# Where transfers for the sums in DRAM stand, and who issues the last features' stores and fetches

## The chip, the core and the metric

The kernel runs on one core of a Trainium2 chip. The core has TensorE (PE, matrix products into PSUM), VectorE (DVE), ScalarE (ACT), GpSimd (POOL) and SyncE (SP); 16 DMA engines move data for it. SP only issues transfers and waits for them, POOL issues transfers and does some elementwise work. Each engine works through its own instructions in order; an instruction that waits holds up all that stand behind it on its engine. The metric is the device time of one execution in microseconds, lower is better. Ahead of the change three runs gave a median of 1498.65 us (1497.84 to 1499.51).

## The reference, cut to what matters

One block on 512 tokens with 16 tokens of meta data ahead of them (528 rows, width 1024), in 32-bit floats:

```python
def swiglu(u, w_gate, w_up, w_down):            # width 1024 -> 2816 -> 1024
    return (jax.nn.silu(u @ w_gate) * (u @ w_up)) @ w_down

h = h + 0.5 * swiglu(rmsnorm(h, ffn1_norm), *ffn1)          # first feed-forward
h = h + hybrid_mixer(rmsnorm(h, mix_norm), ...)             # w_in: q, k, v, gates of both branches
h = h + 0.5 * swiglu(rmsnorm(h, ffn2_norm), *ffn2)          # second feed-forward
return rmsnorm(h, final_norm)[:, 16:]

# hybrid_mixer: retention with 4 heads (key 256, value 512, chunks of 128, decay per head),
# and attention with 8 heads of 128 over keys that an index of 8 small heads selects per query
# (top k); both pass an output matrix and a sigmoid gate, and w_mix_out joins them
```

## The kernel before, in words

**Products.** A matrix product in 32-bit precision is made of three passes: both operands are split into a high part (`whi`, made by ACT, L361) and a rest (`wlo`, made by DVE, L362), and PE sums high times high, high times rest and rest times high. A weight therefore goes the way: load by SP into `raw` (or `wq`, `w`), `whi` by ACT, `wlo` by DVE, PE. A `raw` buffer is free for the next load when DVE has made the last `wlo` from it.

**The two-by-two scheme.** The feed-forwards are computed with sums of weight quarters, so that fewer products are needed (a fast two-by-two scheme). The first feed-forward makes the sums of its weights in SBUF, with DVE (`wsum`, L528 to L534). For the second feed-forward, sums of its gate and up weights (`wsums`) and of its down weights (`dsums`) are made in DRAM by transfers alone, long before they are used. `sum_terms()` gives 48 such transfers in a fixed order: 32 for `wsums` (256x1280 floats each, 1.31 MB), then 16 for `dsums` (512x512, 1.05 MB). I number them t0 to t47. In every group of 16 there are four copies, four that add on arrival, two copies of finished sums and two additions to them, and again two and two. `next_term()` (L335 to L340) issues the next: a plain copy goes to SP's queue, one that adds goes to POOL's. An addition waits until the copy that it adds to has landed; a copy of a sum waits until the additions to that sum have landed.

**Stages.** PE's work comes in steps (a weight to load, a source, a run), and steps_through() runs them as a pipeline with the loads of later steps ahead. In the first feed-forward, steps 0 to 7 are a first downward sum; then come groups of six features each (f0 = 4, 10, 16), of 24 steps (gate and up in alternation, `psqX`, `psqY`, `psqZ` in PSUM, `g` by DVE, L582 to L596) with a downward sum of 8 steps (`psd`, `hT` by DVE, L917) behind each. The downward sum behind f0 = 4 is steps 32 to 39, that behind f0 = 10 is steps 64 to 71; from step `n_busy` = 96 the last downward sum and the projections to values follow (`psvX`, `psvZ`), up to `n_dense` = 157. Then come the retention by heads (`psrk`, `psst`, `psro`, `psrg`), the attention by heads (`psaq`, `psak`, `psao`), the output matrices, and the second feed-forward in six units with features of 14 steps each (`posts_of` puts the work beside them), its downward sums and the final norm.

**Where the terms stand before.** `with_terms(s)` puts a call of `next_term()` behind a step's run. Before, these are steps 8, 16, .. 88 (11 terms), 100, 104, .. 156 (15 terms), and every second one of the retention's steps (24 calls, of which 22 find a term left).

**What sets the order.** PE, ACT and DVE run in the order in which the code is written (BUSY engines in tc.manual_schedule). SP and POOL are ordered by the scheduler. So a moved `next_term()` moves a place in SP's and POOL's order, and PE's order stays as it was.

**Attention and features.** In the attention, the probabilities of a head are turned over by way of DRAM: POOL stores `cross` to `pd`, SP fetches `land` from it, ACT and DVE split it, and PE uses it one head later (L2049 to L2077). In the second feed-forward a unit's features go the same way: `turn()` stores to `hts`, `fetch()` gets `land`, ACT makes `hh`, DVE `hl`, and the downward sum uses them.

Of the kernel before, what the change touches and what calls it, by code (L numbers as in the profile page):

```python
# [81 lines left out]
def kernel(ctx: ExitStack, tc: tile.TileContext, x, meta, g1, wg1, wu1, wd1, gm,  # L82
                      w_in, w_ro, w_ao, w_mo, g2, wg2, wu2, wd2, gf, rope, decay, causal, out):
    nc = tc.nc
# [540 lines left out]
    if True:  # L625
# [33 lines left out]
        half = (slice(0, D // 2), slice(D // 2, D))  # L659
# [614 lines left out]
        n_dense = len(steps)  # L1274
        for i in (*range(8, n_busy, 8), *range(n_busy + 4, n_dense, 4)):
            steps[i] = with_terms(steps[i])
# [682 lines left out]
    with pool("ao") as ao:  # L1959
        vo = [ao.tile([P, AH, S], F32R, tag=f"vo{i}", name="vo") for i in range(2)]  # L1960
        ao_parts = [(vo[0][:, c, :], vo[1][:, c, :]) for c in range(AH)]
        with pool("at") as at:
# [163 lines left out]
            for h in range(AH):  # L2126
                more = h + 1 < AH
                if h == 1:
                    with tc.manual_schedule(engines=BUSY):
                        to_ones = [score(j, q, k) for j in (2, 1, 0, 3)]  # L2130
                        late_v()
                        for to_one in to_ones:
                            to_one()
                elif h:
                    scores(q, k)
# [114 lines left out]
    class Rows:  # L2250
# [67 lines left out]
        def turn(self, c, to, half):  # L2318

            src = self.room[c]  # L2320
            cross = f2["rooms"].tile([P, 1024], F32, tag=f"r{to}", name="cross")[:, : 2 * self.n].rearrange("p (b c t) -> p b c t", t=2, c=32)
            for t in range(2):
                nc.vector.transpose(cross[:, :, :, t], src[:, t].rearrange("p (b k) -> p b k", k=32))  # L2323
            d = hts[self.i % 2, half, : self.n]
            for a in range(4):
                nc.gpsimd.dma_start(d.rearrange("(b i) a e -> a i b e", i=32)[a],  # L2326
                                    cross[32 * a : 32 * a + 32].rearrange("p b c t -> p b (c t)"))

        def fetch(self, land, half):
# [6 lines left out]
            else:  # L2336
                d = d.rearrange("(k p) a e -> p k (a e)", p=P)
            tc.keep_in_program_order(nc.gpsimd.dma_start(t, d))

# [356 lines left out]
    def posts_of(u):  # L2696
# [6 lines left out]
        def put(j, *do):  # L2703
            at[j] += do

        gate_of = lambda c, half: lambda: u.silu(c, half)
        if u is u0:
# [4 lines left out]
            return at  # L2712
        a, b = (4, 6) if u.early else (3, 6)
        if u.early:
# [13 lines left out]
        put(12, lambda: u.gated("E", u.room["E"], u.room["B"], 1), lambda: u.turn("E", "D", 1), lambda: u.fetch("C", 1))  # L2728
        put(13, lambda: u.gated("A", u.d["X"], u.room["A"], 0), lambda: late.append(turn_rest))

# [48 lines left out]
    d = u4.down_steps((last_halves,))  # L2779
    woven(5, {9: d[:1], 12: d[1:2]})  # L2780
    n_units = len(steps)
# [88 lines left out]
```

## Time and profile before

| | us |
|---|---|
| median of three runs | 1498.65 |
| the profiled execution, device time | 1497.69 |
| its span, first to last instruction | 1495.9 |
| PE busy | 1473.3 (98%) |
| DVE busy | 1125.1 (75%) |
| ACT busy | 735.1 (49%) |
| POOL busy | 193.6 (13%) |
| granted TensorE clock, mean | 0.997 |

The times and rows are of one profiled execution; 1497.69 lies 0.96 below the median, inside the spread of the runs. PE is busy nearly all the time, so what counts is what makes PE wait: the waits by engine give that. A row of the timeline tells when an instruction began and how long it took, with the idle time of its engine ahead of it and what ended that in brackets. A DMA issue's last number is the time from the issue to the landing, which includes what is queued ahead of it. In windows, "PEclk" is the granted clock as a share of 2.4 GHz.

### The profile page before, as it was taken

The page shows a single profiled execution, that of the slowest core. Times are in us where ns is not written, and L with a number is a line of the kernel's source. Part 1 is how long each engine was busy: PE and PEld are TensorE (multiplying, and loading weights), DVE is VectorE, ACT ScalarE, POOL GpSimd, SP SyncE. Part 2 cuts the span into 40 slices and gives each one's busy share as a digit, 9 for nine tenths or more (in the row PEclk, how much of TensorE's full clock was granted, in tenths as well). Part 3 has the DMA queues.
Part 4 walks back from the last instruction along what each step waited for, and adds up shares of the span by engine and source line. Part 5 has one row for each costly group of instructions (what it writes and reads, how often), then busy time and mean ns, then how long its engine had stood idle before and what let it go on. Part 6 is the DMA issues. An engine that isn't in the chain of part 4 may idle for free.

```text
span 1495.9 us, 22481 instructions
## 1 busy us (share of the span) xinstructions
PE 1473.3 (98%) x8800; PEld 1306.3 (87%) x8800; DVE 1125.1 (75%) x1736; ACT 735.1 (49%) x1048; POOL 193.6 (13%) x272
## 2 busy tenths in 40 slices
PE   9999999999999999999999999999999999999997
PEld 8999999999887888989898888898888878888885
DVE  4987586686785876777979788778456768897886
ACT  5655254364353444453333437767534645555453
POOL 1000000002210212101101032233001300101110
PEclk9999999999999999999999999999999999999999
DMA  5177533536959879585837644656744656866852
GB/s 171 59 217 204 169 105 103 177 115 166 359 130 357 252 209 269 184 239 165 218 116 211 165 121 119 179 168 178 255 157 141 222 174 217 272 199 222 266 172 99
DMA packets 185594, 281.29 MB, mean 188 GB/s; under 512 B 15120, under 2 KB 113576, under 8 KB 184848
## 3 DMA queue, kind: packets, MB, share of 16 engines
q1 hardware_dynamic: 161856, 209.20, 42.5%
q0 software_dynamic: 20096, 64.35, 18.0%
q10 hardware_dynamic: 3536, 6.31, 1.2%
q8 instruction: 69, 1.13, 0.3%
q14 instruction: 37, 0.30, 0.1%
HBM read 249.66 MB, written 88.88 MB: 226 GB/s over the span
## 4 chain that ended last, share of the span: by engine, by line
PE 81%; DVE 8%; DMA 7%; ACT 2%; issue 2%; SPq 0%; POOLq 0%; POOL 0%; ACTq 0%; DVEq 0%
PE psqX L2368 7%; PE psro L157 6%; PE psqX L157 5%; PE psrg L157 5%; PE psd L157 5%; PE psga L157 3%; PE psat L157 3%; PE psvX L1219 3%; PE psqY L2368 3%; PE psmo L157 3%; PE psak L157 3%; PE psqY L157 3%; PE psaq L157 3%; PE psdX L2430 3%; PE psrk L157 3%; DVE wlo L362 2%
## 5 line engine op out<-in xcount | busy, mean ns | idle before, releaser
L361 ACT ACTIVATE whi<-raw 128x1024 fp32r<-128x1024 f32 (+2 forms) x143 | 134.0, 940 | 117.3 <-PE psd L157 37.2
L362 DVE TENSOR_TENSOR wlo<-raw,whi 128x1024 fp32r<-128x1024 f32 (+2 forms) x143 | 157.8, 1107 | 31.3 <-ACT whi L361 31.2
L362 DVE TENSOR_TENSOR wlo<-wq,whi 128x1024 fp32r<-128x1024 f32 x76 | 92.1, 1216 | 39.6 <-ACT whi L361 39.5
L361 ACT ACTIVATE whi<-wq 128x1024 fp32r<-128x1024 f32 x76 | 80.0, 1060 | 58.3 <-PE psdX L2430 12.7
L157 PE MATMUL psro<-vo,whi 128*128 128x512 f32 x256 | 78.9, 389 | 0.0
L157 PE MATMUL psd<-hl,whi 128*128 128x264 f32 x352 | 71.2, 284 | 0.0
L157 PE MATMUL psd<-hh,wlo 128*128 128x264 f32 x352 | 70.9, 283 | 0.0
L157 PE MATMUL psd<-hh,whi 128*128 128x264 f32 x352 | 70.6, 282 | 0.0
L117 ACT ACTIVATE whi<-raw 128x1024 fp32r<-128x1024 f32 (+1 forms) x44 | 45.4, 1037 | 49.5 <-PE psat L157 17.3
L118 DVE TENSOR_TENSOR wlo<-raw,whi 128x1024 fp32r<-128x1024 f32 (+1 forms) x44 | 53.8, 1222 | 20.6 <-ACT whi L117 20.5
L157 PE MATMUL psqX<-th,whi 128*128 128x264 f32 x216 | 61.3, 284 | 3.8 <-DVE g L596 3.8
L157 PE MATMUL psqX<-tl,whi 128*128 128x264 f32 x216 | 61.1, 283 | 0.0
L157 PE MATMUL psqX<-th,wlo 128*128 128x264 f32 x216 | 61.1, 283 | 0.0
L157 PEld LDWEIGHTS psro<-vo,whi 128*128 128x128 f32 x256 | 48.0, 188 | 10.2
L157 PEld LDWEIGHTS psd<-hh,wlo 128*128 128x128 f32 x352 | 54.4, 188 | 0.0
L157 PEld LDWEIGHTS psd<-hh,whi 128*128 128x128 f32 x352 | 54.3, 188 | 0.0
L157 PEld LDWEIGHTS psd<-hl,whi 128*128 128x128 f32 x352 | 53.9, 188 | 0.0
L2326 POOL DMA_DIRECT2D hts<-cross x40 | 26.5, 693 | 199.5 <-DVE cross L2323 199.4
L361 ACT ACTIVATE whi<-wsum 128x1024 fp32r<-128x1024 f32 x36 | 38.1, 1059 | 28.4 <-PE psd L157 15.0
L157 PE MATMUL psrg<-xh,whi 128*128 128x512 f32 x128 | 50.5, 394 | 0.0
L157 PE MATMUL psrg<-xl,whi 128*128 128x512 f32 x128 | 49.9, 390 | 0.0
L157 PE MATMUL psrg<-xh,wlo 128*128 128x512 f32 x128 | 49.9, 389 | 0.0
(610 smaller groups left out, 4760.4 us busy)
## 6 DMA issues: line engine op xcount, KB each, us to landing
wq<-wsums SPq DMA_DIRECT2D x40, 512.0 KB, 4.5
raw<-in_w_in_dram SPq DMA_DIRECT2D x18, 1024.0 KB, 5.9
raw<-in_w_in_dram SPq DMA_DIRECT2D x33, 512.0 KB, 4.1
w<-in_w_in_dram SPq DMA_DIRECT2D x24, 512.0 KB, 9.0
raw<-in_ffn_w_up_dram SPq DMA_DIRECT2D x11, 1024.0 KB, 5.0
raw<-in_ffn_w_gate_dram SPq DMA_DIRECT2D x10, 1024.0 KB, 5.9
wsums<-in_ffn_w_up_dram POOLq DMA_DIRECT2D x8, 1280.0 KB, 11.1
wsums<-wsums SPq DMA_DIRECT2D x8, 1280.0 KB, 10.8
```

The costliest lines, as they stand in the source:

```text
L117: nc.scalar.activation(hi, src, AF.Copy)
L118: eng.tensor_tensor(lo, src, hi.bitcast(F32), ALU.subtract)
L157: nc.tensor.matmul(o, a[:, k, :], b[:, sl], start=first and k == 0 and i == 0, stop=last and k == nk - 1 and i == 2, skip_group_check=onto)
L361: nc.scalar.activation(hi, src, AF.Copy)
L362: return lambda: nc.vector.tensor_tensor(lo, src, hi.bitcast(F32), ALU.subtract)
L1219: nc.tensor.matmul(d[bank_][t], a, b[:, k, :], start=not onto and j + k + m == 0, stop=j + k == 3 and m == 2, skip_group_check=onto)
L2326: nc.gpsimd.dma_start(d.rearrange("(b i) a e -> a i b e", i=32)[a], cross[32 * a : 32 * a + 32].rearrange("p b c t -> p b (c t)"))
L2368: nc.tensor.matmul(ps[:, t], a, b[:, k, :], start=not onto and j + k + m == 0, stop=j + k == 3 and m == 2, skip_group_check=onto)
L2430: nc.tensor.matmul(ps[:, t], a, b[:, k, :], start=not onto and k + m == 0, stop=k == 1 and m == 2, skip_group_check=onto)
```

## The change

1. In the first feed-forward and the values' stage the terms stand elsewhere: behind steps 32, 34, 36, 38 and 64, 66, 68, 70 (two downward sums, 8 terms) and behind steps 106, 112, .. 154 (9 terms). The retention's 24 calls stay, and issue t17 to t40. A new `next_term()` at the head of each attention head issues t41 to t47.
2. In the second feed-forward's last unit (`i == 5`) the stores of half 0 and both fetches go to SP's queue in place of POOL's, and `turn_rest` runs in step 13 and not behind the next step.
3. In its unit 1 the tiles for the hidden features and half 1 of them come at step 5 in place of 4, and half 0 at step 7 in place of 6.
4. The first downward step that is woven into the last unit stands behind step 10 in place of 9.

```diff
@@ -1272,7 +1272,7 @@
         steps += units[1].steps(units[2], rope_beside(ret_k, slice(0, T))) + [gate_step(OFF_GR + P, 1)]
         steps += units[2].steps(None, rope_beside(ret_q, REAL))
         n_dense = len(steps)
-        for i in (*range(8, n_busy, 8), *range(n_busy + 4, n_dense, 4)):
+        for i in (*range(32, 40, 2), *range(64, 72, 2), *range(n_busy + 10, n_dense, 6)):
             steps[i] = with_terms(steps[i])
         pipe = steps_through(steps)
         with tc.manual_schedule(engines=BUSY):
@@ -2125,6 +2125,7 @@
             pend = None
             for h in range(AH):
                 more = h + 1 < AH
+                next_term()
                 if h == 1:
                     with tc.manual_schedule(engines=BUSY):
                         to_ones = [score(j, q, k) for j in (2, 1, 0, 3)]
@@ -2322,9 +2323,10 @@
             for t in range(2):
                 nc.vector.transpose(cross[:, :, :, t], src[:, t].rearrange("p (b k) -> p b k", k=32))
             d = hts[self.i % 2, half, : self.n]
+            queue = nc.sync if self.i == 5 and half == 0 else nc.gpsimd
             for a in range(4):
-                nc.gpsimd.dma_start(d.rearrange("(b i) a e -> a i b e", i=32)[a],
-                                    cross[32 * a : 32 * a + 32].rearrange("p b c t -> p b (c t)"))
+                queue.dma_start(d.rearrange("(b i) a e -> a i b e", i=32)[a],
+                                cross[32 * a : 32 * a + 32].rearrange("p b c t -> p b (c t)"))
 
         def fetch(self, land, half):
             d = hts[self.i % 2, half, : self.n]
@@ -2335,7 +2337,7 @@
                 t = t.rearrange("p (h k) e -> p h k e", h=2)
             else:
                 d = d.rearrange("(k p) a e -> p k (a e)", p=P)
-            tc.keep_in_program_order(nc.gpsimd.dma_start(t, d))
+            tc.keep_in_program_order((nc.sync if self.i == 5 else nc.gpsimd).dma_start(t, d))
 
         def new_hidden(self, make):
             self.hid = [make(c) for c in "hl"]
@@ -2710,7 +2712,7 @@
             put(2, lambda: split_t(3), lambda: new_t(4), lambda: squares(1), lambda: squares(2), lambda: squares(3), token_norm)
             put(3, load_gf, lambda: split_t(4), u.gates, lambda: late.append(u.turned))
             return at
-        a, b = (4, 6) if u.early else (3, 6)
+        a, b = (5, 7) if u.early else (3, 6)
         if u.early:
             put(a, lambda: prev.new_hidden(plain_tile), lambda: late.append(prev.hidden(1)))
         else:
@@ -2726,7 +2728,7 @@
         put(9, lambda: u.add("E", "X"))
         put(11, lambda: u.add("B", "Y"), lambda: late.append(gate_of("B", 1)))
         put(12, lambda: u.gated("E", u.room["E"], u.room["B"], 1), lambda: u.turn("E", "D", 1), lambda: u.fetch("C", 1))
-        put(13, lambda: u.gated("A", u.d["X"], u.room["A"], 0), lambda: late.append(turn_rest))
+        put(13, lambda: u.gated("A", u.d["X"], u.room["A"], 0), (lambda: turn_rest()) if u.i == 5 else lambda: late.append(turn_rest))
 
         def turn_rest():
             u.turn("A", "B", 0)
@@ -2777,7 +2779,7 @@
         tail_w.extend(split_w(raw[:, i : i + 2, :]) for i in (0, 2))
 
     d = u4.down_steps((last_halves,))
-    woven(5, {9: d[:1], 12: d[1:2]})
+    woven(5, {10: d[:1], 12: d[1:2]})
     n_units = len(steps)
     c0, c1 = [], []
     add_steps(d[2:])
```

The three places that follow are of SP and POOL. An `x3` stands for three equal rows.

SP, first feed-forward, from the last gate and up loads of f0 = 4 over its downward sum into f0 = 10. Before:

```order
L133 DMA raw<-in_ffn_w_gate_dram 128x8x256
L133 DMA raw<-in_ffn_w_up_dram 128x8x256
L339 DMA wsums<-in_ffn_w_gate_dram 256x1280
L133 DMA raw<-in_ffn_w_down_dram 128x6x256 x3
L339 DMA wsums<-in_ffn_w_gate_dram 256x1280
L133 DMA raw<-in_ffn_w_down_dram 128x6x256
L133 DMA raw<-in_ffn_w_gate_dram 128x8x256
L133 DMA raw<-in_ffn_w_up_dram 128x8x256
```

And now:

```order
L133 DMA raw<-in_ffn_w_gate_dram 128x8x256
L133 DMA raw<-in_ffn_w_up_dram 128x8x256
L133 DMA raw<-in_ffn_w_down_dram 128x6x256 x3
L339 DMA wsums<-in_ffn_w_up_dram 256x1280
L133 DMA raw<-in_ffn_w_down_dram 128x6x256
L339 DMA wsums<-in_ffn_w_up_dram 256x1280
L133 DMA raw<-in_ffn_w_gate_dram 128x8x256
L339 DMA wsums<-in_ffn_w_gate_dram 256x1280 x2
L133 DMA raw<-in_ffn_w_up_dram 128x8x256
```

The copies t0 to t2 are gone from among the gate and up loads of f0 = 4 (the last of them is the third row before); all four first copies stand at the downward sum, one more of them ahead of the next gate load and two ahead of the next up load.

SP, end of the retention, with the semaphores that a row waits for (DMAHW: a transfer of SP's, DMASW: one of POOL's). `raw` loads are of the output matrix of the retention and of w_in. Before, around the loads `raw_8365` and `raw_8413`:

```order
L133 DMA raw_8070<-in_w_in_dram 128x8x128 [waits DMAHW1_49,DVE_49]
L133 DMA raw_8163<-in_w_ret_out_dram 128x4x512 [waits DMAHW2_49,DVE_49]
L339 DMA dsums_91<-dsums_91 512x512 [waits DMASW1_49]
L133 DMA raw_8278<-in_w_ret_out_dram 128x4x512 [waits DMAHW6_49,DVE_49]
L133 DMA raw_8365<-in_w_in_dram 128x8x128 [waits DMAHW7_49,DVE_49,Activation_49]
L133 DMA raw_8413<-in_w_in_dram 128x8x256 [waits DMAHW3_49,DMAHW1_49,DVE_49]
L339 DMA dsums_91<-dsums_91 512x512 [waits DMAHW4_49,DMASW6_49]
L133 DMA raw_8491<-in_w_in_dram 128x8x128 [waits DMAHW5_49,DMAHW2_49,DVE_49]
L1441 DMA vraw_8923<-vst_82 128x2048 [waits DVE_49]
```

And now:

```order
L339 DMA dsums_91<-in_ffn2_w_down_dram 512x512 [waits DMAHW1_49]
L133 DMA raw_8061<-in_w_in_dram 128x8x128 [waits DMAHW5_49,DVE_49]
L133 DMA raw_8154<-in_w_ret_out_dram 128x4x512 [waits DMAHW6_49,DMAHW3_49,DVE_49]
L339 DMA dsums_91<-in_ffn2_w_down_dram 512x512
L133 DMA raw_8269<-in_w_ret_out_dram 128x4x512 [waits DMAHW2_49,DVE_49]
L339 DMA dsums_91<-in_ffn2_w_down_dram 512x512
L339 DMA dsums_91<-dsums_91 512x512 [waits DMAHW7_49,DMASW3_49]
L133 DMA raw_8356<-in_w_in_dram 128x8x128 [waits DMAHW0_49,DMAHW3_49,DVE_49,Activation_49]
L133 DMA raw_8404<-in_w_in_dram 128x8x256 [waits DMAHW5_49,DMAHW1_49,DVE_49]
L339 DMA dsums_91<-in_ffn2_w_down_dram 512x512
```

Three copies from the down weights and a copy of a sum (t41, which waits with DMASW3 for an addition on POOL's queue) now stand ahead of the two loads `raw_8356` and `raw_8404`, which were `raw_8365` and `raw_8413`; before, one copy of a sum stood there, whose addition had been issued earlier.

POOL, attention, between the stores of two heads, as a difference:

```order
 L2049 DMA pd<-cross 32x16x128 x2
-L2051 DMA land_9134<-crosst 16x16
+L2051 DMA land_9127<-crosst 16x16
 L1411 DMA vtail<-vd 16x4x128 x3
+L339 DMA dsums<-in_ffn_w_down_dram 512x512
 L2049 DMA pd<-cross 32x16x128
 L1335 TENSOR_TENSOR tmp<-tmp,sin 128x512
```

An addition stands ahead of the next head's stores and of the product with the sine; three more stand at other heads, where before the attention had none, and on SP two copies of sums stand behind the fetches of two heads.

## Rows read from the trace of the kernel before

**Rows 1.** The page's section 1: busy time by engine, share of the span, instructions.
```profile
PE 1473.3 (98%) x8800; PEld 1306.3 (87%) x8800; DVE 1125.1 (75%) x1736; ACT 735.1 (49%) x1048; POOL 193.6 (13%) x272
```

**Rows 2.** Waits of PE: who waited for whom, total us, times, longest us.
```profile
PE psqX L157 <- DVE g L596: 3.8, 2, 2.0
PE psvZ L1219 <- DVE wlo L362: 2.9, 1, 2.9
PE psd L2613 <- DVE hl L362: 2.1, 1, 2.1
PE psqX L2368 <- ACT u L2304: 1.4, 1, 1.4
```

**Rows 3.** Windows of the values' stage: length, busy by engine, PEclk, DMA share, GB/s.
```profile
474.00:478.00 4.00, 1.14 (x6) 0.60 (x4) 3.68 (x4) 2.08 (x2) 0.00 (x0) 1.00 1.03 402
478.00:480.00 2.00, 2.00 (x7) 1.58 (x8) 1.97 (x2) 0.00 (x0) 0.00 (x0) 0.71 1.00 359
480.00:482.00 2.00, 2.00 (x9) 1.15 (x11) 2.00 (x3) 0.00 (x0) 0.00 (x0) 0.50 1.05 366
```

**Rows 4.** SP's timeline, first feed-forward: start, length, what.
```profile
154.04 0.54 SPq L339 DMA_DIRECT2D wsums<-in_ffn_w_gate_dram  x1
164.05 0.37 SPq L133 DMA_DIRECT2D raw<-in_ffn_w_gate_dram  x1
176.51 0.37 SPq L133 DMA_DIRECT2D raw<-in_ffn_w_up_dram  x1
```

**Rows 5.** DMA issues at 80.8, 80.4, 88.7, 91.9 us: KB, us to landing.
```profile
wsums<-in_ffn_w_up_dram SPq DMA_DIRECT2D x1, 1280.0 KB, 7.6
raw<-in_ffn_w_up_dram SPq DMA_DIRECT2D x1, 1024.0 KB, 4.9
wsums<-in_ffn_w_up_dram POOLq DMA_DIRECT2D x1, 1280.0 KB, 11.0
raw<-in_ffn_w_gate_dram SPq DMA_DIRECT2D x1, 1024.0 KB, 10.3
```

**Rows 6.** DVE's timeline (three rows), then ACT's (one), where these loads are used.
```profile
174.20 0.69 DVE L528 TENSOR_TENSOR wsum<-raw 128x512 f32<-128x512 f32 x1 [2.48 <-DMA raw<-in_ffn_w_gate_dram]
179.58 0.77 DVE L917 SCALAR_TENSOR_TENSOR hT<-psd,hT 128x264 f32<-128x264 f32 x2 [0.68 <-PE psd L157]
183.90 0.77 DVE L917 SCALAR_TENSOR_TENSOR hT<-psd,hT 128x264 f32<-128x264 f32 x2 [1.81 <-PE psd L157]
186.84 0.64 ACT L361 ACTIVATE whi<-raw 128x512 fp32r<-128x512 f32 x1 [0.99 <-PE psqZ L157]
```

**Rows 7.** DMA issues in the values' stage at 465.45, 510.88, 512.83 us.
```profile
raw<-in_w_in_dram SPq DMA_DIRECT2D x1, 1024.0 KB, 20.4
wsums<-wsums SPq DMA_DIRECT2D x1, 1280.0 KB, 12.0
raw<-in_w_in_dram SPq DMA_DIRECT2D x1, 1024.0 KB, 27.0
```

**Rows 8.** Retention's end: SP's row, two landings, then ACT, DVE, PE's psst.
```profile
794.80 0.37 SPq L133 DMA_DIRECT2D raw<-in_w_ret_out_dram  x1
raw<-in_w_ret_out_dram SPq DMA_DIRECT2D x1, 1024.0 KB, 8.7
dsums<-in_ffn_w_down_dram POOLq DMA_DIRECT2D x1, 1024.0 KB, 10.2
818.53 1.04 ACT L361 ACTIVATE whi<-raw 128x1024 fp32r<-128x1024 f32 x1
820.75 0.70 DVE L362 TENSOR_TENSOR rqk<-tmp,rqk 128x528 fp32r<-128x528 f32 x1
L1565 PE MATMUL psst<-rqk x30: 170/286/389, 827.1 to 831.1; 128*128 128x512 f32 x6, 128*128 128x400 f32 x6, 128*128 128x272 f32 x6, 128*128 128x256 f32 x6
```

**Rows 9.** The page's section 6: the 512 KB loads of w_in.
```profile
raw<-in_w_in_dram SPq DMA_DIRECT2D x33, 512.0 KB, 4.1
```

**Rows 10.** ACT's timeline in the second feed-forward's unit 1.
```profile
1202.64 0.66 ACT L361 ACTIVATE hh<-land 128x512 fp32r<-128x512 f32 x1 [5.56 <-DMA land<-hts]
```

## The prediction

> **What bounds the kernel now.** First the busy times: PE is busy 98% of the span [rows 1], no other engine comes near, and the clock is full. So the change can only take away time in which PE waits, or add to it. Second, the waits of PE [rows 2]: in the first feed-forward two of about 2 us for `g`, in the values' stage one of 2.9 for a `wlo`, in the second feed-forward one of 1.4 for `u` and, near the end, one of 2.1 for `hl`. These are all that the moved work can win by name. Third, the windows behind the wait in the values' stage [rows 3]: PE works only 1.14 of the 4 us from 474, and then the granted clock falls to 0.71 and 0.50, the lower level of 1.2 GHz, for 4 us. At 2.00 x 0.29 and 2.00 x 0.50 that is 1.6 us more. I put 1.6 behind every new wait that is longer than 2.9 us too.
>
> PE's order is the same but for one pair of steps, so the whole question is when weights land. The timeline of SP and the landings tell that [rows 4, 5]: a 1 MB load alone lands in 4.9 us, a copy of 1.31 MB alone in 7.6, an addition in 11.0, and a load issued beside an addition in 10.3.
>
> **First feed-forward.** Removed: t0 to t2 from among the gate and up loads of f0 = 4. With them go the two waits of [rows 2], if they come from late loads (10.3 in place of 4.9, and DVE in order behind them): 3.8 us, taken in full.
>
> Added: in its downward sum and behind it four copies rather than one, and POOL issues the addition to each as soon as its copy has landed. A last term in this place was t3, issued at 154.04; the next gate load was issued at 164.05 and the next up load at 176.51 [rows 4]. DVE already waits 2.48 us for the gate load, at 174.20 [rows 6], and what it does next is in a fixed order: the `hT` sums that free PE's banks are behind it. Between there and 184 it has only 0.68 + 1.81 = 2.5 us idle.
> - Gate: one more copy (t1) is queued ahead of it on SP. That costs between 0 (it fits in before 164.05) and 12.0, a copy beside an addition [rows 7]. I take 6, nearer to the 7.6 of a copy alone since part of t1 runs ahead of the gate's issue: the gate lands at about 180, and PE is 6 - 2.5 = 3.5 late.
> - Up: behind the gate come t2, t3 and then the load, with the additions to t1 and t2 beside them. A load behind two copies took 20.4 us, a load behind one copy and beside two additions 27.0 [rows 7]. Counted from the gate's landing at 180 the first gives 200, the second with another copy of 7.6 gives 215; a start at 176.51 with 20.4 gives 197. I take 203, nearer to two copies, as the additions start only one by one. ACT wants these weights at 186.84 [rows 6], by now 3.5 later, 190.3; some 2 us lie between ACT and PE (its idle 0.99 and DVE's like). PE waits 203 - 190.3 - 2 = 10.7; ends 5 and 23.
> - With the clock's 1.6: 3.5 + 10.7 + 1.6 - 3.8 = +12.0, ends +1 and +29.
>
> The second four (steps 64 to 70) are additions only; POOL has nothing ahead of them, so they don't run in the second downward sum but at about 162 to 215, as above. The later downward sums get nothing.
>
> A rule stands against that price: the Trainium skill, "DMA: Bandwidth & Descriptors", section "Queues, rings and completion order", says that every DMA engine takes turns packet by packet between the queue rows that have work. By even turns a load beside an addition would take at most twice 4.9, that is 9.8; the trace has 10.3 although the addition ended 7.8 us after the load's issue, so the load got rather less than half. By even turns the up load would be some 5 us earlier, and the whole sum 5 us lower.
>
> **Values' stage.** With 9 terms in place of 15 fewer copies stand ahead of its loads. The wait of 2.9 and its 1.6 of clock [rows 2, 3] should go: -4.5, ends -4.5 and 0 (another transfer lands late there).
>
> **Start of the retention.** t17 stands ahead of a few small loads. I take +0.5, ends 0 and +2, from one 7.6 us copy of which the stage's other work covers most.
>
> **End of the retention.** The third copy is issued right behind the load of 794.80, which landed after 8.7 [rows 8], at 803.5; the copy lands with 7.6 at 811. Its addition on POOL takes 10.2, so 821.3. Only then SP passes t41 and issues `raw_8356`, behind t41's copy: 7.6 and some 1 for the load, 830. ACT split that load at 818.53, DVE ended `rqk` behind it at 821.4 and PE began `psst` with it at 827.1 [rows 8]: 5.7 us of cover. PE is late by 830 - 818.5 - 5.7 = 5.8. The two additions ahead of that one in POOL's queue can add up to 10.2; I take 2. With the clock's 1.6: +9.4; ends 0 (POOL's additions come earlier) and +17. What is queued behind SP's wait is just this: the load of the gate's weights and the next, and behind them the split on ACT and DVE, which hold `psst` and `psro`'s sums.
>
> **Attention.** It gains two copies on SP ahead of 512 KB loads, which land in 4.1 otherwise [rows 9], and four additions beside the stores and fetches of the turned heads. Loads are used as soon as they are there. From below the cost is 0 (PE uses a head's probabilities a head later), from above twice a copy's 7.6 less some 2 of cover each, 11. I take +4: a load behind a copy some 4 late, half of it covered, and as much for an addition beside a fetch.
>
> **Second feed-forward, unit 1.** ACT sat idle for 5.56 until a fetch landed at 1202.64 and only then made what `u` waits for [rows 10]. Now a split stands ahead of that, which gains its 1.04 (a pass of the kind in [rows 8]); but the second fetch stands behind one more weight load on SP, which waits for a buffer. That is one split by ACT and one by DVE, 2.3 together. +1.5; ends -1.4 (the wait of [rows 2] goes) and +2.5.
>
> **Tail.** The stores and fetches of half 0 go to SP, in step 13 itself; the fetch now stands behind the tail's weights. DVE makes `hl` of half 1 behind its work on `hTok` as before, so the 2.1 stays. +0.5; ends -2.1 and +1.5. The Trainium skill, same page, section "Issuing engines are not separate DMA queues", holds that the choice of the issuing engine saves issue time alone; no row here shows more.
>
> **Sum.** 12.0 - 4.5 + 0.5 + 9.4 + 4 + 1.5 + 0.5 = +23.4. On the profiled 1497.69 that is 1521.1; the median stands 0.96 above it. I predict 1521.
>
> **The rivals.**
> - *The loads still come in time* (faster). The downward sums load little (768 KB a step), and if the copies run in that gap, the price at both places is gone. Then -3.8 - 4.5 - 1.4 and at best -2.1 remain: 1487 to 1490. It decides at a gate landing before 177 and an up landing before 190. For it: the first downward sum had one term without a wait of PE. Against it: DVE's 2.48 [rows 6]. 0.12.
> - *Only the first feed-forward pays*: t41's addition is done in time. 12.0 - 4.5 + 0.5 + 4 + 2 = +14, 1512. 0.16.
> - *Only the later stages pay*: the first four copies are absorbed. -3.8 - 4.5 + 0.5 + 9.4 + 4 + 2 = +7.6, 1506. 0.10.
> - *Nothing to be measured*: gains of 8.3 against as much loss. 1498. 0.07.
> - *The terms aren't where the code says*: if POOL held the additions until steps 64 to 70, the up load would lie beside none, land at 197, and 6 us less be lost: 1515, inside my case's range.
>
> **How the numbers follow.** My case, 1513 to 1537, has 0.55. The range 1499 to 1537 takes in it and the two partial cases, and leaves out faster, most of the case at 1498, and some 0.05 above. Faster by over 0.2% (3 us, about what a measurement of this kernel can tell from no change): 0.12; within: 0.07; slower: 0.81.
>
> **What would show it.** In the changed kernel's waits of PE: `g` gone from f0 = 4; a wait of about 3 near 180 and one of about 11 near 192 to 203, with PEclk below 1 behind it; none at 474; one of 6 to 10 at the last head's `psst`, with SP's issue of t41 near the landing of an addition; small ones in the attention. If the landing of the gate and up loads is as before (174 and 181), the largest term is wrong; if SP passes t41 before 812, the second.

## The result, and the profile after

The changed kernel takes 1518.84 us (median of 4 runs, 1517.3 to 1520.39), the kernel before beside it 1498.36 (4 runs, 1497.84 to 1499.51). The ratio is 1.0136 with a 95% interval of 1.0118 to 1.0153: slower by 1.4%. A second measurement, beside three of the later experiments, gave 1.0130 (1.0111 to 1.0148). The prediction was 1521, with 1513 to 1537 for its likeliest case.

The profiled execution of the changed kernel takes 1517.43 with a span of 1515.6, against 1497.69 and 1495.9. The page's busy times, to be held against [rows 1]:

```profile
PE 1480.4 (98%) x8800; PEld 1307.9 (86%) x8800; DVE 1126.7 (74%) x1736; ACT 735.0 (48%) x1048; POOL 188.1 (12%) x266
```

PE's busy time grew by 7.1 us although it does the same work. The lower clock behind its waits, which the windows below show, accounts for about half of that: the mean granted clock is 0.994 in place of 0.997, some 4 us on 1473 (an estimate); the rest of the 7.1 is not traced. The other 12.6 of the 19.7 are waits of PE. The longest of them, to be held against [rows 2] (who waited for whom, total us, times, longest us):

```profile
PE psd L157 <- DVE wlo L362: 6.9, 1, 6.9
PE psqX L2370 <- ACT u L2305: 3.2, 1, 3.2
PE psd L2615 <- DVE hl L362: 2.6, 2, 2.1
PE psst L1565 <- DVE accr L1844: 2.4, 2, 1.7
PE psqX L157 <- DVE g L582: 2.1, 1, 2.1
PE psao L2077 <- DVE ptl L118: 1.8, 4, 0.8
```

The two waits for `g` of [rows 2] and the one of `psvZ` are gone, and so is a shorter one of 1.3 for `psn` ahead of the latter. In their place stand one of 6.9 for a `wlo` in the first feed-forward, one of 2.1 for `g` (now L582), 3.2 in place of 1.4 for `u`, and a row of small ones in the retention (`psst`) and the attention (`psao`, `psS`).

PE's order is the same in both kernels but for one pair of steps in the tail, so the start of the same instruction in both traces tells how late PE is at each place. The stages come out like this:

| from | start before | start after | PE late by | change in the stage | predicted |
|---|---|---|---|---|---|
| first feed-forward, from 6 us (0.8 late there) | 127.48 | 124.39 | -3.1 | -3.9 | -3.8 |
| its downward sum, gate load | 181.54 | 186.82 | 5.3 | +8.4 | +3.5 |
| its next up load | 194.78 | 204.04 | 9.3 | +4.0 | +10.7, and 1.6 of clock |
| values' stage: `psn` | 384.08 | 392.04 | 8.0 | -1.3 | 0 |
| values' stage: `psvZ` | 482.01 | 485.29 | 3.3 | -4.7 | -4.5 |
| start of the retention | 577.94 | 582.63 | 4.7 | +1.4 | +0.5 |
| end of the retention | 829.51 | 837.58 | 8.1 | +3.4 | +9.4 |
| attention | 1061.87 | 1078.80 | 16.9 | +8.9 | +4 |
| second feed-forward, unit 1 | 1207.85 | 1228.19 | 20.3 | +3.4 | +1.5 |
| tail | 1487.32 | 1506.88 | 19.6 | -0.7 | +0.5 |

The largest term first. SP's issues at the first feed-forward's downward sum (start, length, what), in place of [rows 4]:

```profile
153.24 0.57 SPq L339 DMA_DIRECT2D wsums<-in_ffn_w_up_dram  x1
160.85 0.37 SPq L133 DMA_DIRECT2D raw<-in_ffn_w_gate_dram  x1
161.27 8.10 SPq L339 DMA_DIRECT2D wsums<-in_ffn_w_gate_dram  x2
183.77 0.37 SPq L133 DMA_DIRECT2D raw<-in_ffn_w_up_dram  x1
```

POOL's in the same stretch, with what ended the idle time before them:

```profile
158.96 1.01 POOL L339 DMA_DIRECT2D wsums<-in_ffn_w_up_dram  x1 [117.20 <-DMA wsums<-in_ffn_w_up_dram]
166.71 0.90 POOL L339 DMA_DIRECT2D wsums<-in_ffn_w_up_dram  x1 [6.74 <-DMA wsums<-in_ffn_w_up_dram]
185.20 0.87 POOL L339 DMA_DIRECT2D wsums<-in_ffn_w_up_dram  x1 [17.59 <-DMA wsums<-in_ffn_w_gate_dram]
188.14 0.88 POOL L339 DMA_DIRECT2D wsums<-in_ffn_w_up_dram  x1 [2.07 <-DMA wsums<-in_ffn_w_gate_dram]
```

The gate load was issued at 160.85. The addition to t0 had started at 158.96 and the one to t1 followed at 166.71. DVE's rows say when the load was there, and when DVE came to the `wlo` that the longest wait of PE is for:

```profile
181.46 0.69 DVE L528 TENSOR_TENSOR wsum<-raw 128x512 f32<-128x512 f32 x1 [12.95 <-DMA raw<-in_ffn_w_gate_dram]
182.79 0.95 DVE L362 TENSOR_TENSOR wlo<-raw,whi 128x768 fp32r<-128x768 f32 x1
```

That is 12.95 us of waiting where [rows 6] has 2.48. The load took 20.6, by far longer than the 10.3 of [rows 5]; the `wlo` of a down weight for which PE waits, and the `hT` sums, which free PE's banks, stand behind it in DVE's order. The next up load, which waits for the same `wlo` to free a buffer, could then only be issued at 183.77 and landed after 13.4:

```profile
raw<-in_ffn_w_up_dram SPq DMA_DIRECT2D x1, 1024.0 KB, 13.4
```

Windows of the changed kernel (window, length, busy time of PE, PEld, DVE, ACT, POOL, then PEclk, DMA share, GB/s):

```profile
176.00:184.00 8.00, 1.14 (x9) 0.93 (x9) 2.50 (x4) 2.06 (x2) 0.00 (x0) 0.77 1.03 349
184.00:186.00 2.00, 2.00 (x10) 2.00 (x11) 2.00 (x4) 0.05 (x1) 0.80 (x1) 0.50 0.91 356
198.00:201.00 3.00, 0.92 (x7) 0.81 (x7) 3.00 (x5) 1.13 (x3) 0.00 (x0) 0.97 1.03 208
201.00:203.00 2.00, 2.00 (x11) 2.00 (x11) 2.00 (x4) 0.97 (x2) 0.00 (x0) 0.50 0.95 250
831.00:835.00 4.00, 2.35 (x11) 1.64 (x10) 3.97 (x8) 1.06 (x1) 0.00 (x0) 1.00 1.05 381
1226.00:1228.00 2.00, 2.00 (x6) 1.56 (x5) 1.90 (x3) 2.00 (x3) 0.00 (x0) 0.50 0.30 37
```

In the first, PE works 1.14 us of 8 while the DMA engines are full (1.03). Behind it the clock is 0.50, the lower level of 1.2 GHz, as in [rows 3]; behind the second wait (198 to 201) again. At 831, in the retention, waits that are shorter leave it at 1.00. The last is of the second feed-forward, behind 3.2 us of waiting: 0.50.

### The profile page after: what moved, and what is told of

It is laid out like the page before. It is cut to its first block, busy times and chain, and to the rows that moved or that the text cites. A ratio compares the mean times of both kernels' runs of the same rounds, so it can differ in the third digit from the quotient of the medians.

```text
span 1515.6 us, 22484 instructions
## 1 busy us (share of the span) xinstructions
PE 1480.4 (98%) x8800; PEld 1307.9 (86%) x8800; DVE 1126.7 (74%) x1736; ACT 735.0 (48%) x1048; POOL 188.1 (12%) x266
## 4 chain that ended last, share of the span: by engine, by line
PE 79%; DMA 8%; DVE 7%; issue 2%; ACT 2%; SPq 1%; POOL 0%; POOLq 0%; ACTq 0%; DVEq 0%
PE psd L157 7%; PE psqX L2370 7%; PE psqX L157 7%; PE psvX L1219 4%; PE psro L157 4%; PE psqY L157 3%; PE psrq L157 3%; PE psat L157 3%; PE psqY L2370 3%; PE psmo L157 3%; PE psrg L157 3%; PE psrk L157 2%; PE psga L157 2%; PE psvY L1219 2%; PE psdX L2432 2%
## 5 line engine op out<-in xcount | busy, mean ns | idle before, releaser
L361 ACT ACTIVATE whi<-raw 128x1024 fp32r<-128x1024 f32 (+2 forms) x143 | 134.2, 941 | 125.3 <-PE psd L157 34.1
L157 PE MATMUL psro<-vo,wlo 128*128 128x512 f32 x128 | 49.8, 389 | 0.0
## 6 DMA issues: line engine op xcount, KB each, us to landing
wsums<-in_ffn_w_up_dram POOLq DMA_DIRECT2D x8, 1280.0 KB, 13.4
```

The costliest lines, as they stand in the source:

```text
L157: nc.tensor.matmul(o, a[:, k, :], b[:, sl], start=first and k == 0 and i == 0, stop=last and k == nk - 1 and i == 2, skip_group_check=onto)
L361: nc.scalar.activation(hi, src, AF.Copy)
```

## The experiments

All times are medians, each with its ratio to the kernel before in the same call. The kernel before took 1498.18 beside the first eight terms alone, the additions left out, the terms later and unit 1 as before; 1497.34 beside the attention's additions left out, the two kernels with 9 terms and the changed kernel again; 1495.55 beside the last four. In the last all its runs but one lie between 1492.4 and 1499.7, so that differences of a tenth of a per cent stay open. Against the changed kernel, which ran in the second of these calls alone, the others are compared by their ratios.

**One part alone: the first eight terms.** The kernel before, with

```diff
-        for i in (*range(8, n_busy, 8), *range(n_busy + 4, n_dense, 4)):
+        for i in (*range(32, 40, 2), *range(64, 72, 2), *range(72, n_busy, 8), *range(n_busy + 4, n_dense, 4)):
```

> The kernel before with one edit: t0 to t7 stand behind steps 32, 34, 36, 38 and 64, 66, 68, 70 of the first feed-forward (as in the changed kernel) and t8 to t10 stay at steps 72, 80, 88; nothing else of the program is touched. Theory (the four copies and their additions at the downward sum hold up the next gate and up loads; that is a loss by itself): PE's start after that place was 9.3 - 0.7 = 8.5 us later in the changed kernel, so about 1498.5 + 8.5 = 1507, with a wait of PE psd for wlo near 180 of about 7 us and none for g at 103 and 126. Rival (the loss is given back later, since PE's delay gives the loads of the values' stage and the retention more time): the wait at 475 shrinks or goes and the time is 1500 to 1503.

Measured: 1503.87, ratio 1.0046 (1.0022 to 1.0069), 5.7 us (3.3 to 10.3 by the interval). Its waits of PE:

```profile
PE psd L157 <- DVE wlo L362: 5.7, 1, 5.7
...
PE psvZ L1219 <- DVE wlo L362: 1.6, 1, 1.6
```

The wait near 180 is there by itself, with one of 1.3 for `g` near 209. From 6 us to 216 us PE loses 5.9 us, in the changed kernel's first trace 8.6, in its second 5.9; behind 475 the wait was 1.6 in place of 2.9, and 1.1 us is given back there. The time lies between the two theories' ranges, nearer to the rival's (up to 1503) than to 1507, and its interval takes in both. The trace shows the loss by itself, and little of it given back.

**The additions left out.** The changed kernel, with t4 to t7 not issued:

```diff
+    left_out = [terms[i] for i in range(4, 8)]
...
-            dst, src, add = terms.pop(0)
+            term = terms.pop(0)
+            if any(term is t for t in left_out):
+                return
+            dst, src, add = term
```

> The changed kernel with the additions t4 to t7 left out (the first four terms that add on arrival are not issued, so the sums lack a part); the copies t0 to t3 stand where they stood. Theory (the additions on POOL's queue, which start as each copy lands, take the DMA engines from the gate load behind them: it was issued at 160.9 and landed 181.4, 1.5 after the second addition landed at 179.9): without them the gate load lands by 172, PE's waits near 180 and 198 (6.9 and 2.1 us) and the low clock behind them go, and 8.4 + 4.0 = about 12 us are gone, 1506 to 1508. Rival (the copies on SP's own queue ahead of and behind the load are enough): the gate load still lands after 178 and the time is 1516 to 1519.

Measured: 1504.54, ratio 1.0048 (1.0031 to 1.0066), against 1.0130 with them: 12.3 us (13.2 by the first measurement's 1.0136). The same two copies t2 and t3 land like this (KB, median us), first in the changed kernel, then without the additions:

```profile
wsums<-in_ffn_w_gate_dram SPq DMA_DIRECT2D x2, 1280.0 KB, 24.8
```

```profile
wsums<-in_ffn_w_gate_dram SPq DMA_DIRECT2D x2, 1280.0 KB, 11.8
```

And DVE took up the gate load without waiting for it, 7.6 after its issue at 160.09, so that it landed within 7.6 at most:

```profile
167.67 0.68 DVE L532 TENSOR_TENSOR wsum<-raw 128x512 f32<-128x512 f32 x1
```

The instruction of PE that starts at 204.04 in the changed kernel, and at 194.78 before, starts at 190.82 here. So the copies on SP's queue alone cost nothing here, four of them with two loads among them and one behind: what costs is the additions, which start of themselves as each copy lands. The theory holds.

Why an addition holds up a load so much, the DMA queues show. While the gate load of the changed kernel lay beside additions (166.8 to 179.8), then in this kernel (160.1 to 167.6); q0 is POOL's queue, q1 SP's (packets, MB, share of the 16 engines' time):

```profile
q0 software_dynamic: 425, 2.01, 77.5%
q1 hardware_dynamic: 931, 1.07, 25.7%
```

```profile
q1 hardware_dynamic: 1419, 2.86, 100.4%
```

SP's queue moved 1.07 MB in 13 us beside the additions and 2.86 MB in 7.5 us without them. Beside them it still moved more than twice as many packets as POOL's, but had a quarter of the time: a packet of an addition kept an engine busy for about 0.38 us, one of SP's for 0.06 (estimates from these rows: the share of the time, times the window, times 16 engines, divided by the packets).

**The attention's additions left out.** The same edit with `(42, 43, 46, 47)`:

> The changed kernel with the four additions of the attention left out (t42, t43, t46 and t47 are not issued, so the second and fourth sums of the down weights lack a part); the three copies stand where they stood. Theory (the additions, 10 to 12 us each on the DMA engines, hold up the fetches of the turned heads, which took 7 to 9 us beside them in place of 3 to 4, and PE's start was 7 us later between 1015 and 1065, where the last two lie): 1518.8 - 7 = about 1512, and no wait of psao for ptl over 0.5. Rival (the two copies on SP, which stand behind the fetches and ahead of the weight loads, are the cause): no more than 2 us are gone, 1517.

Measured: 1509.59, ratio 1.0086 (1.0069 to 1.0103), 7.4 less than with them. The fetches of a turned head in the changed kernel, beside the last addition; then before; then here, beside none (KB, median us to landing):

```profile
dsums<-in_ffn_w_down_dram POOLq DMA_DIRECT2D x1, 1024.0 KB, 11.9
land<-pd SPq DMA_DIRECT2D x2, 256.0 KB, 8.8
```

```profile
land<-pd SPq DMA_DIRECT2D x2, 256.0 KB, 2.7
```

```profile
land<-pd SPq DMA_DIRECT2D x2, 256.0 KB, 2.7
```

8.8 in place of 2.7. Against the changed kernel's run in the same call, PE's start was 0.0 apart at 837 and 7.8 earlier at 1064. The additions are the cause. Against the kernel before, PE is 8.0 late here at 831 and 7.2 at 1062, so that the two copies on SP, which I had weighed equally, cost nothing that this trace shows.

**The same terms later.** `next_term()` taken out of the heads' loop and put into the loop over the column blocks of the attention's output matrix:

> The changed kernel with t41 to t47 issued behind the attention, one at each column block of the attention's output matrix, in place of one at each attention head. That takes t41's copy, which waits for an addition, from ahead of two weight loads at the end of the retention, and two copies and four additions out of the attention. Theory (they cost about 3 us at the retention's end and 8.9 us in the attention, where PE got later by so much): 1518.8 - 12 = about 1507, with at most 3 more if the output matrix stage pays for them. Rival (the attention's delay comes from elsewhere, or the copies cost as much behind the attention, where the second feed-forward's first weights are loaded): 1514 to 1519.

Measured: 1513.44, ratio 1.0116 (1.0091 to 1.0141). In the trace 2.9 us go at the retention's end (SP no longer waits with t41 there) and 8.0 in the attention, as expected, but 9 of these 11 come back within 70 us, most of it at one place:

```profile
PE psao L2077 <- ACT pth L117: 5.2, 1, 5.2
```

A copy, issued at 1044.20, now stands ahead of the last head's fetches, and an addition, issued at 1046.73, lies beside them; which of the two makes them late was not tried. The theory held for what was taken out, the rival for where it was put.

**Unit 1 as before.** The changed kernel with

```diff
-        a, b = (5, 7) if u.early else (3, 6)
+        a, b = (4, 6) if u.early else (3, 6)
```

> The changed kernel with the posts of the second feed-forward's unit 1 as before (hidden tiles and half 1 at step 4, half 0 at step 6). Theory (the later steps let one more weight load go ahead of the second fetch, so that u, which ACT makes behind hh, comes late: PE waits 3.2 in place of 1.4, and the clock falls to 0.50 behind it): the PE wait for u is back at 1.4 and 3.4 us are gone, 1515.4. Rival (the longer wait comes from the whole stage lying 17 us later against its transfers, not from the posts): 1518 to 1519 with a wait of 3 for u.

Measured: 1513.59, ratio 1.0112 (1.0081 to 1.0143), 2.7 us less than the changed kernel's 1.0130 by the ratios, whose intervals overlap. The trace is plainer; its wait for `u`:

```profile
PE psqX L2370 <- ACT u L2305: 0.9, 1, 0.9
```

0.9 in place of 3.2, and PE's lead over the changed kernel grows by 3.9 us at just this place. In the changed kernel ACT's row, to be held against [rows 10], is

```profile
1222.39 0.66 ACT L361 ACTIVATE hh<-land 128x512 fp32r<-128x512 f32 x1 [6.50 <-DMA land<-hts]
```

This speaks for the posts, but doesn't show that they are the whole. With the posts as changed the wait for `u` was 3.4 in the second trace of the changed kernel, 2.4 and 2.0 in the two kernels without additions and 1.7 with the attention's terms later; with the posts as before it runs from 0.9 here to 2.2 in the kernels below. What else sets it was not tried.

**A version that beats both, first try.** The one gain of the change lies in the values' stage. The kernel before, with 9 terms there and the last four at the mix output product:

```diff
-        for i in (*range(8, n_busy, 8), *range(n_busy + 4, n_dense, 4)):
+        for i in (*range(8, n_busy, 8), *range(n_busy + 10, n_dense, 6)):
...
-        steps += [(*mo_raw(c), lambda w, lower, c=c: mo_run[0](c, w, lower)) for c in range(KD)]
+        steps += [(*mo_raw(c), lambda w, lower, c=c: (mo_run[0](c, w, lower), next_term())) for c in range(KD)]
```

> The kernel before with three of its places changed: the values' stage has 9 terms as in the changed kernel (steps n_busy + 10, + 16, ..) in place of 15, the first feed-forward keeps its 11, the retention's 24 calls all find a term (before: 22), and the last four terms (two copies, two additions) are issued by the steps of the mix output product. Theory (the one gain that the changed kernel showed is the values' stage: the waits at 382 and 475 and the low clock behind the latter, 1.3 + 4.7 = 6 us; a few terms more are free where no load is needed at once): 1492 to 1495 where the kernel before has 1498. Rival (every moved term costs elsewhere about what it gained): 1497 to 1501.

Measured: 1512.54, ratio 1.0099 (1.0084 to 1.0114). PE was 7.6 us early at 482, so the gain is there (some of it is a wait for `g` that is missing from this trace, though the first feed-forward's terms stand as before); but then come these waits of PE:

```profile
PE pspv L1586 <- ACT wt L1343: 12.4, 1, 12.4
PE psro L157 <- ACT vo L361: 3.7, 1, 3.7
```

With fewer terms ahead the retention begins with four additions, all issued within 3 us, where the kernel before has two. What lay beside them (KB, us to landing):

```profile
wsums<-in_ffn_w_up_dram POOLq DMA_DIRECT2D x4, 1280.0 KB, 23.0
raw<-in_w_in_dram SPq DMA_DIRECT2D x1, 1024.0 KB, 34.1
```

A load of 1 MB takes 34.1. The terms at the mix output product cost nothing. My theory missed that the later terms change their kind at every place when their count ahead changes.

**The same, by the gate loads.** `range(12, n_busy, 8)` in place of `range(8, n_busy, 8)`:

> As values_9_terms, and the 11 terms of the first feed-forward four steps later (steps 12, 20, .. 92 in place of 8, 16, .. 88), so that a copy follows a gate load and its addition lies beside the next up load. Theory (an addition beside any gate or up load makes that land in 10 in place of 5, and DVE and PE wait for it in either case): the two waits for g of 2 us stay in another place, time as values_9_terms within 2. Rival (up loads have cover that gate loads lack): those waits go and it is 4 lower.

Measured: 1515.27, ratio 1.0115 (1.009 to 1.0141). Both theories fail in part:

```profile
PE psqX L157 <- DVE g L582: 3.3, 2, 2.2
```

The waits at 103 and 126 went, and others came near 137 and 310. Nor did it save the 4 us: 1.0115 against 1.0099. What makes the difference is seen in the next kernel, which shares this place.

**The smallest moves.** From that, three kernels with the first two terms at steps 12 and 20, all else as before; then with t17 two steps later too (`124` to `126`); then, in place of that, two terms fewer in the values' stage.

> The kernel before with two terms moved: t0 and t1 stand behind steps 12 and 20 in place of 8 and 16, so that each copy follows a gate load and its addition lies beside the up load behind; t2 to t47 stay. Theory (an up load has cover that a gate load lacks, and the third addition was free where it lay, in the downward sum): the two waits for g near 103 and 126 (3.8 us) go and nothing takes their place, 1494.5 where the kernel before has 1498.2. Rival (what the waits hide comes up elsewhere, as in values_9_terms_by_gate, where a wait came near 139): 1497 to 1499.

Measured: 1495.7, ratio 1.0002 (0.9989 to 1.0016). No change, by the rival: a wait for `g` of 2.5 stands near 136 in place of the two, and the one in the values' stage stays:

```profile
PE psqX L157 <- DVE g L582: 2.5, 1, 2.5
...
PE psvZ L1219 <- DVE wlo L362: 2.0, 1, 2.0
```

SP's and POOL's issues there, and DVE's row behind the second addition:

```profile
100.17 0.38 SPq L133 DMA_DIRECT2D raw<-in_ffn_w_up_dram  x1
110.37 0.37 SPq L133 DMA_DIRECT2D raw<-in_ffn_w_gate_dram  x1
...
121.57 0.37 SPq L133 DMA_DIRECT2D raw<-in_ffn_w_up_dram  x1
```

```profile
101.78 1.02 POOL L339 DMA_DIRECT2D wsums<-in_ffn_w_up_dram  x1 [61.12 <-DMA wsums<-in_ffn_w_up_dram]
120.54 0.89 POOL L339 DMA_DIRECT2D wsums<-in_ffn_w_up_dram  x1 [17.74 <-DMA wsums<-in_ffn_w_up_dram]
```

```profile
133.25 0.69 DVE L528 TENSOR_TENSOR wsum<-raw 128x512 f32<-128x512 f32 x1 [4.60 <-DMA raw<-in_ffn_w_up_dram]
```

The first addition (101.78) began when the up load of 100.17 was on its way and was all but over when the gate load was issued at 110.37: nothing waited. The second (120.54) began 1.0 us ahead of an up load, DVE waited 4.60 for it, and PE with it. So here it is no matter of gate or up: an addition of 10 to 11 us nearly fills the time from one load to the next; the one that began behind a load's issue was free, the one that began ahead of it was not.

> As two_terms_by_gate, and t17 behind step 126 in place of 124 (two steps after n_busy + 28), so that its copy stands behind a pair of weight loads of the values' stage and no longer ahead of them. Theory (the wait of 2.9 near 475 and the low clock behind it, 4.6 us in all, come from this one copy queued ahead of the late load): 3.8 + 4.6 = 8.4 less than the kernel before, 1490. Rival (it takes fewer terms, as with 9 of them, since the additions beside do it too): the wait stays above 1.5 and the time is 1493 to 1495.

Measured: 1494.43, ratio 0.9986 (0.9973 to 1.0). The wait of `psvZ` is gone, with one copy moved by two steps; PE gains 2.3 us there on the kernel above. The one for `g` is as in that kernel, 2.6. The two differ in nothing else, so in these traces it was that one copy. The kernel has the lowest median of all here, 1.1 us below the kernel before, at the edge of what can be told.

> As two_terms_by_gate, and the values' stage has 13 terms (none behind steps 124 and 128), all later terms two calls later, so that the retention begins with the copies t24 and t25 and every one of its 24 calls finds a term. Theory (the order of the terms at the retention's edges decides: with copies at its start and four additions not at once, the waits of 12.4 and 3.7 us of values_9_terms don't come): 1491 to 1495. Rival (any shift of the retention's terms makes one of its loads late): over 1498 with a wait of pspv, psst or psro above 2.

Measured: 1504.64, ratio 1.0064 (1.0043 to 1.0084), by the rival. A copy now stands ahead of `u`, the retention's decay, beside two additions; PE's wait and DVE's row:

```profile
PE psst L1565 <- DVE tmp L1569: 11.5, 1, 11.5
```

```profile
581.58 1.17 DVE L1569 TENSOR_TENSOR tmp<-psst,u 128x512 f32<-128x512 f32 x2 [17.24 <-DMA u<-in_decay_dram]
```

**The tail's edits on top.** The kernel with three terms moved, with half 0's stores and both fetches by SP, `turn_rest` at once and the weave at step 10:

> As three_terms_moved, and the changed kernel's edits of the second feed-forward's last unit (half 0's stores and both fetches by SP, turn_rest in its own step, the first woven downward step behind step 10), without those of unit 1. Theory (in the changed kernel PE's start fell back by 0.7 us in the tail, so they are worth that or nothing): as three_terms_moved within 1. Rival (the fetches queue behind the tail's weights and cost 1.5): 1 to 2 slower.

Measured: 1495.07, ratio 0.9994 (0.998 to 1.0009): within 1 of the kernel without them, as expected; they are worth nothing that can be told, either way.

**The changed kernel again**, beside the kernels of the second call:

> The changed kernel again, on the same chip and beside the same runs of the kernel before as the three that follow. Every theory: 1517 to 1520, ratio about 1.0136; the length of the wait near 180 may differ by 2 us from run to run, since it hangs on how the transfers share the DMA engines.

Measured: 1517.02, ratio 1.0130. The wait near 180 was 5.7 in place of 6.9. At the end of the retention PE waited 3.4 at once, and there the clock fell too:

```profile
833.00:836.00 3.00, 2.70 (x6) 2.15 (x7) 2.96 (x6) 0.54 (x1) 0.00 (x0) 0.50 0.91 302
```

This trace and those of the experiments that leave a part of the changed kernel as it is show how far the table's numbers move from one execution to the next. The first feed-forward, from 6 to 216 us, cost 8.6 us in the table's trace, 5.9 in this one, and 5.9, 5.2 and 4.4 in three others; the end of the retention 3.5, 5.4, and 2.8 to 6.3; the attention 8.7, 8.0, and 8.6 and 11.0. So a stage's number from one trace holds to some 2 to 4 us.

## Why the prediction was right, point by point

- **What bounds the kernel**: right. PE's order and work are the same, and where it falls behind it is at its waits and in the low clock behind them.
- **First feed-forward**: +12.0 predicted, +8.5 measured by the table, 4.4 to 5.9 in four other traces. The gains were right (3.9). The gate load was put at 180 and taken up at 181.46, which looks near; but PE waited 6.9 and lost 1.5 of clock in place of 3.5. The first term that was mis-sized is "I take 6" for what the gate load loses. With the first waits gone PE and the load's issue both came 3 us earlier (160.85 in place of 164.05), so the load should have landed at 177. It took 20.6 in place of the 10.2 of [rows 4, 6], 10.4 more; less the 2.5 of idle time that is 7.9, and 6.9 was waited. The second is "I take 203" for the up load, which DVE took up at 197.18 and which cost 2.1 and 1.6 of clock in place of 10.7 and 1.6. I counted copies and additions one behind the other from the gate's landing. But the up load was issued only at 183.77, for lack of a buffer, and by then t2 and t3 had little more to go: POOL's additions to them began at 185.20 and 188.14, as they landed. And PE itself was 5.4 late by then. The mechanism I shared out between SP's copies and POOL's additions; the run without the additions shows that it is the additions.
- **The rule on taking turns** (the Trainium skill, "DMA: Bandwidth & Descriptors", section "Queues, rings and completion order"): taken as even shares, as the prediction's estimate took it, it doesn't fit here. The gate load of 1 MB lay beside one or two additions from 160.85 to 179.9 and landed 1.5 behind them; without them it took 7.6 at most. Turns by packet are not even shares of the time where the packets differ as they do here, 0.38 us against 0.06.
- **Second four terms**: right. POOL issued them at 158.96 to 188.14, not in the second downward sum.
- **Values' stage**: -4.5 predicted, -4.7 measured, and -1.3 at `psn`, which I had left out.
- **Start of the retention**: +0.5 predicted, +1.4 measured, inside its ends of 0 and 2.
- **End of the retention**: +9.4 predicted, +3.4 measured. The chain was right: SP issued t41 at 822.42, at the landing of the addition, and the two loads behind it; ACT waited for both:

```profile
800.43 0.51 SPq L339 DMA_DIRECT2D dsums<-in_ffn_w_down_dram  x1
822.42 0.48 SPq L339 DMA_DIRECT2D dsums<-dsums  x1
823.06 1.12 SPq L133 DMA_DIRECT2D raw<-in_w_in_dram  x2
```

```profile
829.33 1.06 ACT L361 ACTIVATE whi<-raw 128x1024 fp32r<-128x1024 f32 x1 [5.61 <-DMA raw<-in_w_in_dram]
833.49 1.06 ACT L361 ACTIVATE whi<-raw 128x1024 fp32r<-128x1024 f32 x1 [3.10 <-DMA raw<-in_w_in_dram]
```

  The step that failed is the start of the chain, "the copy lands with 7.6 at 811". In the changed kernel that copy was issued at 800.43 and the addition behind it at 810.87; the load ahead had landed at 807.1, so the copy landed some 3 us behind that load and not 7.6. The rows had shown it: the 7.6 of [rows 5], which the prediction calls that of a copy alone, is counted from an issue 0.42 behind a load's; that load landed at 85.3 (80.4 and 4.9) and the copy at 88.4 (80.8 and 7.6), 3.1 behind it. And as the waits were short, no clock was lost in the table's trace (1.00 in the window at 831); in the second one it was, and the stage cost 5.4.
- **Attention**: +4 predicted, +8.9 measured, inside its ends of 0 and 11. The cause was half wrong: it is the additions beside the fetches, and hardly the copies ahead of the weight loads.
- **Unit 1**: +1.5 predicted, +3.4 measured, beyond its upper end of 2.5. The wait grew by 1.8 to 3.2, near the 1.5; but the term left out the clock, which the prediction adds behind every wait over 2.9, and PEclk fell to 0.50 behind this one.
- **Tail**: +0.5 predicted, -0.7 measured; the tail's edits alone gave no difference. The -0.7 is one of the clock: behind the wait of 2.1 for `hl` PEclk was 0.50 from 1466 to 1468 in the kernel before, and 1.00 behind the same wait in the changed kernel (1484.6 to 1488.5).
- The sum of 23.4 was near 19.7 in part by luck: two terms that were too large (the up load by 8.3, the retention's end by 6.0) stood against three that were too small (the gate load and the attention by 4.9 each, unit 1 by 1.9).
- The two gains, 3.8 in the first feed-forward and 4.5 in the values' stage, can be had apart from the loss only in part: in the smallest moves 2.5 to 2.6 of the first came back near 136.

## What to carry to other kernels

A transfer that starts of itself when another lands belongs in the plan with its own time and place: here the additions, and not the copies that the code places, made the loads late. Look for the queue whose engine has nothing else ahead of it; that is where a moved call doesn't stay where the code puts it. And when the count of such terms ahead changes, every later place gets another kind of transfer: check each of them: at the start of the retention two additions cost PE no wait in the kernel before, and four cost 12 us.

## What the runs showed of the hardware that was not expected

- A 1 MB load beside one addition took 10.3 us [rows 5], behind a copy and beside two additions 20.6, and at the start of the retention beside four additions 34.1; alone 4.9. By the first of these a load has about a third of its pace beside an addition (an estimate): 7.8 of the 10.3 us lay beside it, and the other 2.5 are half of the 4.9 that it takes alone.
- Four copies in a row on SP's queue, with two loads among them, one behind and no addition, cost PE nothing.
- The length of a wait of PE doesn't tell by itself whether the clock falls behind it. In the kernel before the two waits for `g`, of 1.8 and 2.0, left it at 1.00, and one of 2.1 at 1462 was followed by 0.50; in the changed kernel one of 2.1 at 198, some 15 us after a longer one, was followed by 0.50, and one of 2.1 at 1482 by 1.00. The wait of 2.5 near 134 in the kernel with two terms moved left it at 1.00 (137 to 139), and its wait of 1.2 for `psn` at 381 was followed by 0.50 (384 to 386), where the same wait of 1.3 in the kernel before left 1.00. What makes the difference was not tried.
